# One layer of a hybrid encoder block on one core: TensorE's instructions fixed in program order, the recurrence's norm moved beside the next pair's chain, its output kept split, and the merge's gate blocks fetched ahead

## The chip, the core and the metric

The kernel runs on one core of a Trainium2 chip. The metric is the device time of one execution in microseconds. The kernel before took 1546.63 us (median of three runs, 1545.62 to 1550.25).

## What is computed

One layer over a sequence of 256 positions and a width of 2048, all in float32:

```
proj = rms_norm(x) @ w_in               # columns: SGU u, v | RWKV features | gate_a | gate_b
y_a  = sgu_mixer(u, v)                  # layer norm over 1024 columns, then 128x128 mixing per group
y_b  = rwkv_mixer(features)             # 16 heads of 64: a forward and a backward scan
       # o = group norm(o_f + o_b);  y_b = (o + bonus) * (sigmoid(g_lo) @ g2)
x    = x + (sigmoid(gate_a) * (y_a @ w_proj_a) + sigmoid(gate_b) * (y_b @ w_proj_b)) @ w_out
x    = x + (silu(conv3(rms_norm(x) @ w_gate)) * (rms_norm(x) @ w_up)) @ w_down
out  = rms_norm(x)
```

The scan is done in chunks of 64 positions: a 64x64 triangular system is inverted for each chunk, head and direction, and a short chain of small products carries the state from chunk to chunk.

## The kernel before

All large products run the same way. A weight tile (`raw`, 256 KB) comes from HBM; ScalarE rounds it (L271) and VectorE takes the remainder (L272), so that `hl` holds the weight as two parts; the activations are split in the same way. TensorE then issues, for each block of 128 weight rows, one matmul of 512 columns (L294) and one of 256 (L298). Four such pairs of matmuls make a chunk. `push` queues the chunks of a product, `advance(n)` issues the next n of them and splits the weights of three chunks ahead (`HL_AHEAD`), and `done` is what follows a product's last matmul: `evac_sum` takes the sum out of PSUM with one ScalarE copy (L310) and one VectorE addition (L311) into one of two `ev` buffers.

The small work is written as generators, and `run` lays chunks between their steps: a generator's `yield` says how much of the chunks should pass before its next step. The order is: the SGU (`sgu`), rates and operands of head pair 0, and then a loop over the pairs. In step p stand side by side the chain of pair p (`rwkv_chain`), the inverse of pair p+1 (`rwkv_inverse`) and the rates of pair p+2, and after them the norm of pair p (`rwkv_norm`) and the operands of pair p+2. `parts` splits a tile into `bs`, and `head_sums` (L642) sums it over a head with two matmuls into the one-bank PSUM tile `ms`. The large products between them are the projections and the gates; a gate block is written to DRAM by `keep` (L978, `spill`, through POOL's DMA queue).

This text is not the final order. A scheduler at build time moves instructions on every engine's queue, TensorE's included: where its cost table says that a small matmul's operand will not be ready, it takes a large matmul that stands later in the program. On the chip each engine then works its queue strictly in that order.

After the loop comes the merge: the outputs `yb` of the eight pairs are split into `ybs`, and for each of 16 column tiles `done_b` reads the gate block back (`sab`, L1070, through SP's queue), combines it and splits the result into `mg`. Then follow the output product, a norm (`sumsq_rstd`), the gate and up products and the down product.

Of the kernel before, what the change touches and what calls it, by code (L numbers as in the profile page):

```python
# [10 lines left out]
F32 = mybir.dt.float32  # L11
F32R = mybir.dt.float32r
I32 = mybir.dt.int32
AF = mybir.ActivationFunctionType
ALU = mybir.AluOpType
PSUM = bass.MemoryType.PSUM

P = 128
T = 256
D = 2048  # L20
KT = D // P
# [3 lines left out]
NP = RW // P  # L25
# [12 lines left out]

J0 = 4
WARM = 12  # L40
GY, TY, CY = 1.5, 2.5, 1.0
INV_Y = 4 * GY + 1.2 + 6 * TY + 2
CHAIN_Y = 12 * CY
SY = 1
NORM_Y = 3 + 2 * SY
# [74 lines left out]
    return out  # L120


@with_exitstack
def hybrid_kernel(ctx: ExitStack, tc: tile.TileContext, xT, w_in, w_pa, w_pb, w_out, w_g, w_u, w_d,
                  cols, consts, lora, sgu_wT, sgu_b, norm_f, out):
    nc = tc.nc
    V, A, PE, G = nc.vector, nc.scalar, nc.tensor, nc.gpsimd

    cpool = ctx.enter_context(tc.tile_pool(name="cpool", bufs=1))
    ps_mm = ctx.enter_context(tc.tile_pool(name="ps_mm", bufs=2, space=PSUM))  # L130
# [7 lines left out]
    def col(name, i):  # L138
        o, _ = COLS[name]
        return colt[:, o + i:o + i + 1]  # L140
# [41 lines left out]
    def split(dst, src):  # L182

        A.copy(dst[:, 0], src)
        V.tensor_tensor(out=dst[:, 1], in0=src, in1=dst[:, 0].bitcast(F32), op=ALU.subtract)
# [134 lines left out]
    drp = ctx.enter_context(tc.tile_pool(name="drp", bufs=1, space=bass.MemoryType.DRAM))  # L320
    es_mid, es_h, es_ya, es_f, es_h2, es_mg = (ExitStack() for _ in range(6))
    mid = es_mid.enter_context(tc.tile_pool(name="mid", bufs=1))
    hp = es_h.enter_context(tc.tile_pool(name="hp", bufs=1))
    fpool = es_f.enter_context(tc.tile_pool(name="fpool", bufs=1, side="right"))


    hp.tile([P, 8], F32, name="pad_h")
    h = [hp.tile([P, 2, T], F32R, name=f"h{k}") for k in range(KT)]
    hact = lambda k: h[k]
    yb = [mid.tile([P, T], F32, name=f"yb{p}") for p in range(NP)]  # L330


    fps = [fpool.tile([P, T + 2], F32, name=f"fp{i}") for i in range(2)]
# [276 lines left out]
    rp = es_r.enter_context(tc.tile_pool(name="rp", bufs=1, reuse_waits="tile"))  # L610
# [4 lines left out]
    rt = lambda name, shape, bufs=1: rp.tile([P] + shape, F32, name=name, tag=name, bufs=bufs)  # L615
# [30 lines left out]
    def rwkv_rates(p):  # L646

        k, v3, r, _ = feats[p]

        lr = rt("kd", [4, P])  # L650
        G.dma_start(lr, lora[p][:, 0:4])
        lgr = rt("Em", [4, P])[:, 0:2]
        G.dma_start(lgr, lora[p][:, 4:6])
        yield LY
        lw = rp.tile([P, 4, P], F32R, name="lw", tag="lw")
        A.copy(lw, lr)
        lg = rp.tile([P, 3, P], F32R, name="lg", tag="lg", bufs=3)
        A.copy(lg[:, 0::2], lgr)
        V.tensor_tensor(out=lg[:, 1], in0=lgr[:, 0], in1=lg[:, 0].bitcast(F32), op=ALU.subtract)
        V.tensor_tensor(out=lg[64:96, 2], in0=lgr[64:96, 1], in1=lg[64:96, 2].bitcast(F32), op=ALU.subtract)  # L660
        V.tensor_tensor(out=lw[C:P], in0=lr[C:P], in1=lw[C:P].bitcast(F32), op=ALU.subtract)
        yield 1
        tw = rt("tw", [2, T])
        ta = rt("ta", [2, T])
        for d in range(2):
            lp = ps_g.tile([P, 512], F32, name="gp", tag="gp")
            for i in range(2):
                for o in range(2):
                    PE.matmul(lp[:, i * T:(i + 1) * T], lw[:, 2 * i + d], xlo[i][d][:, o], start=(o == 0), stop=(o == 1))
            A.activation(tw[:, d], lp[:, 0:T], AF.Tanh, scale=0.5, bias=hb[:, d * NP + p:d * NP + p + 1])  # L670
            A.activation(ta[:, d], lp[:, T:2 * T], AF.Tanh, scale=0.5,
                         bias=hb[:, (2 + d) * NP + p:(2 + d) * NP + p + 1])
# [12 lines left out]
        ss = rt("hs", [T])
        ty = rt("tmp", [T], 3)
        kk = rt("kk", [T])
        A.activation(ss, k, AF.Square, scale=col("k_k", p))
        sp = parts(ss)
        yield SY  # L690
        sp = head_sums(sp)
        V.tensor_scalar(out=ss, in0=sp[:, 0:T], scalar1=1e-24, scalar2=None, op0=ALU.max)
        yield 1
        rsqrt(ty, ss, kk)
        V.scalar_tensor_tensor(out=kk, in0=k, scalar=col("k_k", p), in1=ty, op0=ALU.mult, op1=ALU.mult)
        yield 1
        bc = lambda a: a[:, None, :].to_broadcast([P, 2, T])

        kd = rt("kd", [4, P]).rearrange("p (d a) b -> p d (a b)", d=2)
        V.tensor_scalar(out=kd, in0=ta, scalar1=col("k_a", p), scalar2=ka2[:, p:p + 1], op0=ALU.mult, op1=ALU.add)  # L700
        V.tensor_tensor(out=kd, in0=kd, in1=bc(k), op=ALU.mult)
        V.scalar_tensor_tensor(out=ta, in0=ta, scalar=1.0, in1=bc(kk), op0=ALU.add, op1=ALU.mult)
        yield 1
        rates[p] = (L, Em, kk, kd, ta, lg)

    def rwkv_operands(p):

        k, v3, r, _ = feats.pop(p)
        L, Em, kk, kd, ta, lg = rates.pop(p)
        AR, PB = ARs[p % 2], PBs[p % 2]  # L710
        cv = lambda a: a.rearrange("p d (c j) -> p d c j", j=C)
        bcc = lambda a: a.rearrange("p (c j) -> p c j", j=C)[:, None].to_broadcast([P, 2, NC, C])
# [38 lines left out]
        V.tensor_tensor(out=bv.rearrange("p (a b) -> p a b", a=2), in0=bp[:, 0:T].rearrange("p (a b) -> p a b", a=2),  # L751
                        in1=v3f[:, :, 0:P], op=ALU.mult)
        yield 1
        heads[p] = (BK, UV, ZR, bv, lg)

    def rwkv_inverse(p):

# [41 lines left out]
        Tc = rt("Tc", [2, NC, 32], 2)  # L799
        V.transpose(out=Tc, in_=FQ[:, :, :, 1, :])  # L800
        keys_by_token(1)
        yield 1.2
        for l in range(2):
            xp = ps_t.tile([P, 512], F32, name="tp", tag="tp")
            xv = xp[:, 0:256].rearrange("p (d c k) -> p d c k", d=2, c=NC)
# [66 lines left out]
        yield 1  # L872

    def rwkv_chain(p):
        BK, UV, ZR, bv, lg = heads[p]
        Gs, Qf = solved.pop(p)
        AR, PB = ARs[p % 2], PBs[p % 2]

# [61 lines left out]
        outs[p] = O  # L940

    def rwkv_norm(p):
        BK, UV, ZR, bv, lg = heads.pop(p)
        O = outs.pop(p)

        mp = parts(O)
        yield SY
        mp = head_sums(mp)
        V.scalar_tensor_tensor(out=O, in0=mp[:, 0:T], scalar=-1.0 / C, in1=O, op0=ALU.mult, op1=ALU.add)
        yield 1  # L950
        sq2 = rt("tmp", [T], 3)
        A.activation(sq2, O, AF.Square)
        vp = parts(sq2)
        yield SY
        vp = head_sums(vp)
        ss2 = sq2
        ty2 = rt("tmp", [T], 3)
        tt2 = rt("tmp", [T], 3)
        V.tensor_scalar(out=ss2, in0=vp[:, 0:T], scalar1=1.0 / C, scalar2=GN_EPS, op0=ALU.mult, op1=ALU.add)
        yield 1  # L960
        rsqrt(ty2, ss2, tt2)
        V.tensor_tensor(out=O, in0=O, in1=ty2, op=ALU.mult)
        V.scalar_tensor_tensor(out=O, in0=O, scalar=col("gn_g", p), in1=bv, op0=ALU.mult, op1=ALU.add)
        gp2 = ps_ms.tile([P, 512], F32, name="ms", tag="ms")
        PE.matmul(gp2[:, 0:T], lg[:, 0], gsp[:, 0], start=True, stop=False)
        PE.matmul(gp2[:, 0:T], lg[:, 0], gsp[:, 1], start=False, stop=False)
        PE.matmul(gp2[:, 0:T], lg[:, 1], gsp[:, 0], start=False, stop=False)
        PE.matmul(gp2[:, 0:T], lg[0:96, 2], gst[0:96], start=False, stop=True)
        V.scalar_tensor_tensor(out=yb[p], in0=O, scalar=col("gn_b", p), in1=gp2[:, 0:T], op0=ALU.add, op1=ALU.mult)
        yield 1  # L970


    spill = {}
# [37 lines left out]
    for p in range(-1, NP):  # L1011
# [3 lines left out]
            pair_feats(p + 3)  # L1015
        push_fill(FILLS[p + 2])
        side, then = [], []
        if p >= 0:
            then.append((rwkv_norm(p), NORM_Y))
        if p < 0 or p + 1 == NP:  # L1020
            side.append((rwkv_inverse(p + 1), INV_Y) if p < 0 else (rwkv_chain(p), CHAIN_Y))
# [2 lines left out]
        if p + 2 < NP:  # L1024
# [11 lines left out]

    pools.update(raw=ctx.enter_context(tc.tile_pool(name="raw2", bufs=RAW2, reuse_waits="tile", side="right")),
                 ahead=RAW2 - 2)  # L1040
    xp_ = ctx.enter_context(tc.tile_pool(name="x2p", bufs=1, reuse_waits="tile", side="right"))
# [6 lines left out]
    h2 = [h2p.tile([P, 2, T], F32R, name=f"h2{m}") for m in range(KT)]  # L1048
    rstd2 = xp_.tile([P, T], F32, name="rstd2")
    mgr = es_mg.enter_context(tc.tile_pool(name="mgr", bufs=1, reuse_waits="tile", side="right"))  # L1050
    es_x = ExitStack()
    mgp = es_x.enter_context(tc.tile_pool(name="mgp", bufs=1, reuse_waits="tile"))
    mg = [mgr.tile([P, 2, T], F32R, name=f"mg{m}") for m in range(KT)]
    mgp.tile([P, 8], F32, name="pad_y")
    ybs = [mgp.tile([P, 2, T], F32R, name=f"ybs{p}") for p in range(NP)]
    for p in range(NP):
        split(ybs[p], yb[p])

    x2 = {}

    def load_x(m):
# [4 lines left out]
    def done_b(m, ps):  # L1066
        if m >= KT - X_AHEAD:
            load_x(m - KT + X_AHEAD)
        sab = mgp.tile([P, 2, T], F32, name="sab", tag="sab", bufs=4)
        nc.sync.dma_start(sab, spill[m])  # L1070
        sa, sb = sab[:, 0], sab[:, 1]
        V.scalar_tensor_tensor(out=sb, in0=sb, scalar=1.0, in1=evac_sum(ev, ps), op0=ALU.add, op1=ALU.mult)
        V.tensor_tensor(out=sa, in0=sa, in1=sb, op=ALU.add)
        split(mg[m], sa)
# [12 lines left out]
        last_d = push_tok(w_d[n], FT, lambda k: lt["act"][k], lambda t, ps, n=n: lt["d"](n, t, ps),  # L1087
                          LAG if n == ND - 1 else 0)
    finish(last_b)
    es_x.close()  # L1090
    es_mid.close()

    def sumsq_rstd(pool, dst, n_eps):
# [186 lines left out]
```

## Time and profile before

| | |
|---|---|
| median of three runs | 1546.63 us |
| the profiled execution | 1550.3 us |
| its span, first to last instruction | 1548.2 us |
| TensorE busy | 1525.0 us, 99% |
| VectorE busy | 1214.3 us, 78% |
| ScalarE busy | 925.0 us, 60% |
| granted TensorE clock, mean | 0.997 |

How to read it: TensorE's busy time includes the overlap of pipelined matmuls, so 99% does not mean that no time can be saved; the distance from one matmul's start to the next one's tells more. A wait is shown with the instruction that ended it.

### The profile page before, as it was taken

What the parts mean: (1) busy time and instruction counts of PE and PEld (TensorE: products, weight loads), DVE (VectorE), ACT (ScalarE), POOL (GpSimd) and SP (SyncE); (2) the same over time, 40 slices, a digit from 0 to 9 for tenths busy, and PEclk for the clock granted to TensorE, in tenths of its full rate; (3) what the DMA queues carried; (4) which work ended last, traced back from release to release, by engine and by line L of the source; (5) the groups of instructions that cost most, each with busy time, mean ns of one, the idle gap of its engine ahead of it and who ended that gap; (6) DMA issues with size and microseconds to landing.
All of it is one profiled execution on the core that took longest, in us unless ns stands there. A gap on an engine that the chain in (4) does not pass through costs nothing.

```text
span 1548.2 us, 34103 instructions
## 1 busy us (share of the span) xinstructions
PE 1525.0 (99%) x12680; PEld 1310.8 (85%) x12680; DVE 1214.3 (78%) x2496; ACT 925.0 (60%) x1946; POOL 38.1 (2%) x63
## 2 busy tenths in 40 slices
PE   9999999999999999989999999999999999999997
PEld 8888888888788878878888888888888888888886
DVE  8979998899889997678778777777777777555544
ACT  7767666665665664556665666665656666544442
POOL 0000000000000000000000000000000000000000
PEclk9999999999999999999999999999999999999999
DMA  8555453443443333587655555555555556766663
GB/s 282 187 176 186 155 165 123 132 133 133 134 141 121 125 100 129 178 272 244 207 189 183 189 191 190 190 189 192 190 190 188 192 188 217 230 193 194 194 175 110
DMA packets 148165, 274.65 MB, mean 177 GB/s; under 512 B 17056, under 2 KB 19232, under 8 KB 147872
## 3 DMA queue, kind: packets, MB, share of 16 engines
q1 hardware_dynamic: 145296, 265.14, 52.7%
q0 software_dynamic: 2560, 7.34, 1.5%
q8 instruction: 99, 1.62, 0.4%
q14 instruction: 66, 0.54, 0.1%
q10 hardware_dynamic: 144, 0.01, 0.0%
HBM read 266.13 MB, written 6.29 MB: 176 GB/s over the span
## 4 chain that ended last, share of the span: by engine, by line
PE 83%; issue 9%; DVE 4%; DMA 1%; ACT 1%; POOL 0%; SPq 0%; DVEq 0%; ACTq 0%; POOLq 0%
PE mm L294 40%; PE mm L298 21%; PE pd L232 5%; PE pd L230 5%; PE pd L231 5%; PE gp L770 1%; PE tp L818 1%; DVE hl L272 1%; PE ms L642 1%; DMA sab<-spill 1%; DVE FQ L796 1%; PE tp L808 1%; DMA spill<-ev 1%; PE cc L901 0%; ACT hl L271 0%
## 5 line engine op out<-in xcount | busy, mean ns | idle before, releaser
L294 PE MATMUL mm<-h,hl 128*128 128x512 f32 x2624 | 930.1, 395 | 0.0
L272 DVE TENSOR_TENSOR hl<-raw,hl 128x512 fp32r<-128x512 f32 x960 | 656.7, 691 | 218.9 <-ACT hl L271 215.5
L271 ACT CAST hl<-raw 128x512 fp32r<-128x512 f32 x960 | 593.5, 621 | 380.3 <-PE mm L298 162.8
L298 PE MATMUL mm<-h,hl 128*128 128x256 f32 x2624 | 740.6, 282 | 1.5 <-DVE hl L272 1.3
L294 PEld LDWEIGHTS mm<-h,hl 128*128 128x128 f32 x2624 | 492.8, 188 | 103.8
L298 PEld LDWEIGHTS mm<-h,hl 128*128 128x128 f32 x2624 | 495.9, 189 | 3.0 <-DVE hl L272 2.1
L310 ACT COPY ev<-mm 128x256 f32<-128x256 f32 x196 | 73.1, 373 | 125.2 <-PE mm L298 123.3
L231 PE MATMUL pd<-hl,act 128*128 128x512 f32 x352 | 136.9, 389 | 0.0
L230 PE MATMUL pd<-hl,act 128*128 128x512 f32 x352 | 136.9, 389 | 0.0
L232 PE MATMUL pd<-hl,act 128*128 128x512 f32 x352 | 136.9, 389 | 0.0
L311 DVE TENSOR_TENSOR ev<-mm,ev 128x256 f32<-128x256 f32 x196 | 82.9, 423 | 44.6 <-ACT ev L310 43.2
L294 PE MATMUL mm<-mg,hl 128*128 128x512 f32 x256 | 90.7, 395 | 0.0
L231 PEld LDWEIGHTS pd<-hl,act 128*128 128x128 f32 x352 | 66.1, 188 | 13.8
L232 PEld LDWEIGHTS pd<-hl,act 128*128 128x128 f32 x352 | 66.1, 188 | 13.8
L230 PEld LDWEIGHTS pd<-hl,act 128*128 128x128 f32 x352 | 66.1, 188 | 13.6
L298 PE MATMUL mm<-mg,hl 128*128 128x256 f32 x256 | 72.1, 282 | 0.0
L294 PEld LDWEIGHTS mm<-mg,hl 128*128 128x128 f32 x256 | 48.1, 188 | 9.6
L294 PE MATMUL mm<-ybs,hl 128*128 128x512 f32 x128 | 46.1, 401 | 4.0 <-DVE ev L311 3.4
L298 PEld LDWEIGHTS mm<-mg,hl 128*128 128x128 f32 x256 | 48.4, 189 | 0.0
L294 PE MATMUL mm<-ya,hl 128*128 128x512 f32 x128 | 47.7, 404 | 0.0
L1161 ACT ACTIVATE gt<-cp,colt 128x256 f32<-128x256 f32 x44 | 26.5, 602 | 19.4 <-DVE cp L1159 19.4
L298 PE MATMUL mm<-ybs,hl 128*128 128x256 f32 x128 | 36.8, 287 | 0.0
(292 smaller groups left out, 1430.5 us busy)
## 6 DMA issues: line engine op xcount, KB each, us to landing
raw<-in_w_in_dram SPq DMA_DIRECT2D x304, 256.0 KB, 2.9
raw<-in_w_g_dram SPq DMA_DIRECT2D x176, 256.0 KB, 2.7
raw<-in_w_u_dram SPq DMA_DIRECT2D x176, 256.0 KB, 2.8
raw<-in_w_d_dram SPq DMA_DIRECT2D x176, 256.0 KB, 3.0
raw<-in_w_out_dram SPq DMA_DIRECT2D x64, 256.0 KB, 3.0
raw<-in_w_pa_dram SPq DMA_DIRECT2D x32, 256.0 KB, 2.9
raw<-in_w_pb_dram SPq DMA_DIRECT2D x32, 256.0 KB, 4.3
spill<-ev POOLq DMA_DIRECT2D x32, 128.0 KB, 3.1
```

Source lines behind the costliest of these rows:

```text
L230: PE.matmul(ps, a[:, 0, ts], w[:, 0], start=(k == 0), stop=False)
L231: PE.matmul(ps, a[:, 0, ts], w[:, 1], start=False, stop=False)
L232: PE.matmul(ps, a[:, 1, ts], w[:, 0], start=False, stop=(k == nk - 1))
L271: A.copy(hl[:, 0, :m], raw[:, s0:s0 + m])
L272: V.tensor_tensor(out=hl[:, 1, :m], in0=raw[:, s0:s0 + m], in1=hl[:, 0, :m].bitcast(F32), op=ALU.subtract)
L294: PE.matmul(ps[:, 0:512], hl[:, 0, j], a.rearrange("p a t -> p (a t)"), start=(k == 0), stop=False)
L298: PE.matmul(ps[:, 0:256], hl[:, 1, j], a[:, 0], start=False, stop=(k == job["nk"] - 1))
L310: A.copy(t, ps[:, 256:512])
L311: V.tensor_tensor(out=t, in0=ps[:, 0:256], in1=t, op=ALU.add)
L642: PE.matmul(ps[:, 0:T], bones, b[:, o], start=(o == 0), stop=(o == 1))
L770: PE.matmul(gps[hh][:, c * P:(c + 1) * P], BK[rows, d, c, hh:hh + 2, :].rearrange("p a b -> p (a b)"), AR[rows, d, c].rearrange("p a b -> ...
L1161: A.activation(gt, b[:, 1:T + 1], AF.Identity, scale=col("cw1", f), bias=col("cb", f))
```

## The change

1. A class `InOrder` wraps `matmul` and `transpose`. Each TensorE instruction gets a dependency on the one before it, with no semaphore, so the scheduler keeps TensorE's queue in the order of the program. (All TensorE instructions now carry the line of the wrapper, L133.)
2. The norm of pair p no longer follows chain p; it runs in the next step, beside the chain of pair p+1. The norm of the last pair still follows its chain.
3. The norm writes its result to `O` and splits it at once into `ybs[p]`; the merge no longer splits eight tiles. The 256 KB of gate LoRA weights (`lgr`) are fetched and split in the norm instead of in the rates.
4. The gate blocks for the merge are fetched on POOL's queue instead of SP's, three tiles ahead, from a pool that is opened when the pairs' pools close. The DMA scratch is set to 8192 bytes.
5. Two steps of the inverse get other weights for `run`: 1.25 instead of 1.5 for each of the four products at its start, and 2.2 instead of 1.2 after the first transposition.

```
-GY, TY, CY = 1.5, 2.5, 1.0
-INV_Y = 4 * GY + 1.2 + 6 * TY + 2
+GY, TY, CY = 1.25, 2.5, 1.0
+INV_Y = 4 * GY + 2.2 + 6 * TY + 2
...
+class InOrder:
...
+    def _next(self, op, *args, **kw):
+        tc = self.tc
+        traced = tc.nc.cur_bb.bb.instructions
+        n = len(traced)
+        op(*args, **kw)
+        for ins in traced[n:]:
+            if self.last is not None:
+                tc.add_manual_dep(
+                    ins, self.last.name,
+                    mybir.DependencyInfo(mybir.DependencyClass.NoSync, mybir.DependencyReason.DATA),
+                    reason="order")
+            self.last = ins
...
-    V, A, PE, G = nc.vector, nc.scalar, nc.tensor, nc.gpsimd
+    V, A, G = nc.vector, nc.scalar, nc.gpsimd
+    PE = InOrder(tc)
...
-    yb = [mid.tile([P, T], F32, name=f"yb{p}") for p in range(NP)]
+    ybs = [mid.tile([P, 2, T], F32R, name=f"ybs{p}") for p in range(NP)]
...
     def rwkv_norm(p):
+        bv = heads.pop(p)[3]
         O = outs.pop(p)
+        lgr = rt("lgr", [2, P])
+        G.dma_start(lgr, lora[p][:, 4:6])
...
-        V.scalar_tensor_tensor(out=yb[p], in0=O, scalar=col("gn_b", p), in1=gp2[:, 0:T], op0=ALU.add, op1=ALU.mult)
+        V.scalar_tensor_tensor(out=O, in0=O, scalar=col("gn_b", p), in1=gp2[:, 0:T], op0=ALU.add, op1=ALU.mult)
+        split(ybs[p], O)
...
-        if p >= 0:
+        if p > 0:
+            side.append((rwkv_norm(p - 1), NORM_Y))
+        if p == NP - 1:
             then.append((rwkv_norm(p), NORM_Y))
...
+    def load_sab(m):
+        if m < KT:
+            sab[m] = sap.tile([P, 2, T], F32, name="sab", tag="sab", bufs=4)
+            G.dma_start(sab[m], spill[m])
+
+    for m in range(3):
+        load_sab(m)
...
-    for p in range(NP):
-        split(ybs[p], yb[p])
...
-        sab = mgp.tile([P, 2, T], F32, name="sab", tag="sab", bufs=4)
-        nc.sync.dma_start(sab, spill[m])
-        sa, sb = sab[:, 0], sab[:, 1]
+        load_sab(m + 3)
+        s_ = sab.pop(m)
+        sa, sb = s_[:, 0], s_[:, 1]
```

What the scheduler makes of it shows in TensorE's queue. First place: the mean of the SGU's layer norm (`ms<-acc`), which follows the last of the eight v products. `h_96` to `h_111` are the 16 blocks of one product. TensorE before:

```order
L294 MATMUL mm<-h_99,hl 128x512
L298 MATMUL mm<-h_99,hl 128x256
L294 MATMUL mm<-h_100,hl 128x512
L298 MATMUL mm<-h_100,hl 128x256
L294 MATMUL mm<-h_101,hl 128x512
L298 MATMUL mm<-h_101,hl 128x256
L294 MATMUL mm<-h_102,hl 128x512
L298 MATMUL mm<-h_102,hl 128x256
L472 MATMUL ms<-acc,cst 128x256
```

TensorE of the change, at the same `ms<-acc`:

```order
L133 MATMUL mm<-h_110,hl 128x512
L133 MATMUL mm<-h_110,hl 128x256
L133 MATMUL mm<-h_111,hl 128x512
L133 MATMUL mm<-h_111,hl 128x256
L133 MATMUL ms<-acc,cst 128x256
L133 MATMUL mm<-h_96,hl 128x512
L133 MATMUL mm<-h_96,hl 128x256
```

Before, 14 large matmuls of the next product (blocks 96 to 102) stood ahead of the sum; now it stands directly behind the product that feeds it. In the whole queue, 270 large matmuls stood ahead of it and now 256; ahead of the first transposition of the SGU (`sgt`) 375 and now 352; ahead of the last sum of the second norm (`ms<-sqn`) 3463 and now 3456; ahead of the first `ms<-bs` of pair 0's operands 880 and now 872. In the loop over the pairs, the small products that follow an operand from VectorE or ScalarE have up to 7 large matmuls fewer ahead of them in a step with an odd pair, and up to 11 fewer in one with an even pair, counted from the step's first large matmul.

Second place: where the chain of one pair (`cc`, `oc`), the products at the start of the next pair's inverse (`gp<-AR,BK`) and the norm's sums meet. TensorE before:

```order
L889 MATMUL cc<-ZR,Gs 64x64 x3
L642 MATMUL ms<-bs,bones 128x256
L889 MATMUL cc<-ZR,Gs 64x64
L770 MATMUL gp<-AR_1689,BK 128x128 x2
L642 MATMUL ms<-bs,bones 128x256
L770 MATMUL gp<-AR_1689,BK 128x128 x5
L965 MATMUL ms<-gsp,lg 128x256
L966 MATMUL ms<-gsp,lg 128x256
L967 MATMUL ms<-gsp,lg 128x256
L968 MATMUL ms<-gst,lg 128x256
L770 MATMUL gp<-AR_1689,BK 128x128
```

TensorE of the change, there:

```order
L133 MATMUL mm<-ya_134,hl 128x512
L133 MATMUL mm<-ya_134,hl 128x256
L133 MATMUL cc<-ZR,Gs 64x64 x4
L133 MATMUL gp<-AR_1689,BK 128x128 x8
L133 MATMUL mm<-h_96,hl 128x512
L133 MATMUL mm<-h_96,hl 128x256
```

Groups of one kind now stand together. Over the whole queue, 214 stretches of small matmuls between large ones became 180, 328 changes of the tile shape (128x128, 64x128, 128x64, 64x64, 32x32) became 279, and `gp<-AR,BK` comes in 16 pieces instead of 31.

Third place: POOL's queue at the merge, DMA alone. `spill` followed by a number is one gate block in DRAM. POOL before:

```order
L978 DMA spill_9354<-ev 128x256 x2
L978 DMA spill_9591<-ev 128x256 x2
L978 DMA spill_9796<-ev 128x256 x2
L978 DMA spill_10069<-ev 128x256 x2
L1152 MEMSET cp_11858 128x258
```

POOL of the change:

```order
L1006 DMA spill_9572<-ev 128x256 x2
L1006 DMA spill_9806<-ev 128x256
L1076 DMA sab<-spill_2218 128x512
L1076 DMA sab<-spill_2937 128x512
L1076 DMA sab<-spill_3658 128x512
L1006 DMA spill_9806<-ev 128x256
L1076 DMA sab<-spill_3958 128x512
L1006 DMA spill_10066<-ev 128x256 x2
L1076 DMA sab<-spill_4828 128x512
```

The last three writes of gate blocks now stand behind three and four fetches of 256 KB each.

## Rows read from the trace of the kernel before

**Rows 1.** The page: busy us of the engines, share of the span, instructions

```profile
PE 1525.0 (99%) x12680; PEld 1310.8 (85%) x12680; DVE 1214.3 (78%) x2496; ACT 925.0 (60%) x1946; POOL 38.1 (2%) x63
```

**Rows 2.** Window in the pairs: length, busy us of each engine, clock, DMA share, GB/s

```profile
520.00:540.00 20.00, 19.94 (x226) 16.03 (x226) 18.02 (x46) 12.27 (x34) 0.54 (x1) 1.00 0.27 95
```

**Rows 3.** Timeline of TensorE in the pairs: start us, duration, line, tiles

```profile
279.31 0.39 PE L294 MATMUL mm<-ya,hl 128*128 128x512 f32 x1
279.76 0.38 PE L642 MATMUL ms<-bs,bones 128*128 128x256 f32 x1
279.98 0.28 PE L298 MATMUL mm<-ya,hl 128*128 128x256 f32 x1
280.10 0.39 PE L294 MATMUL mm<-ya,hl 128*128 128x512 f32 x1
280.32 0.28 PE L642 MATMUL ms<-bs,bones 128*128 128x256 f32 x1
280.44 0.28 PE L298 MATMUL mm<-ya,hl 128*128 128x256 f32 x1
...
281.72 0.38 PE L642 MATMUL ms<-bs,bones 128*128 128x256 f32 x1
282.03 0.33 PE L889 MATMUL cc<-ZR,Gs 64*64 64x64 f32 x2
...
284.97 0.50 PE L294 MATMUL mm<-h,hl 128*128 128x512 f32 x1
285.31 0.28 PE L298 MATMUL mm<-h,hl 128*128 128x256 f32 x1
285.43 0.39 PE L294 MATMUL mm<-h,hl 128*128 128x512 f32 x1
285.66 0.28 PE L298 MATMUL mm<-h,hl 128*128 128x256 f32 x1
```

**Rows 4.** Waits of TensorE, by line and releaser: total us, times, longest

```profile
PE tp L808 <- DVE Tc L800: 3.0, 5, 0.9
...
PE gp L770 <- DVE BK L720: 1.1, 1, 1.1
```

**Rows 5.** Timeline of TensorE at the merge: matmuls that waited

```profile
663.25 0.38 PE L298 MATMUL mm<-h,hl 128*128 128x256 f32 x1 [1.32 <-DVE hl L272]
...
668.02 0.47 PE L294 MATMUL mm<-ybs,hl 128*128 128x512 f32 x1 [0.57 <-DVE ybs L185]
...
679.97 0.64 PE L294 MATMUL mm<-ybs,hl 128*128 128x512 f32 x1 [3.39 <-DVE ev L311]
```

**Rows 6.** Timeline at the SGU's mean and at its first transposition

```profile
54.94 0.42 DVE L415 TENSOR_TENSOR acc<-acc,vu 128x256 f32<-128x256 f32 x1
55.42 0.70 PE L472 MATMUL ms<-acc,cst 128*128 128x256 f32 x2
...
74.31 1.09 ACT L494 ACTIVATE vu<-vu,colt 128x256 f32<-128x256 f32 x2
74.97 0.44 PE L497 MATMUL sgt<-cst,vu 128*128 128x128 f32 x2
```

**Rows 7.** Timeline at pair 0's first products and operands; [wait <-releaser]

```profile
169.77 0.49 PE L770 MATMUL gp<-AR,BK 64*128 64x128 f32 x2 [1.07 <-DVE BK L720]
...
172.84 0.41 DVE L185 TENSOR_TENSOR bs<-hs,bs 128x256 fp32r<-128x256 f32 x1
```

**Rows 8.** Window of 4 us behind the wait of 3.39 us at the merge

```profile
680.00:684.00 4.00, 4.00 (x14) 3.42 (x15) 3.22 (x8) 1.32 (x3) 0.00 (x0) 0.57 0.72 222
```

**Rows 9.** The chain that ended last, at the merge: start, us, transfer

```profile
654.14 7.93 DMA spill<-ev
...
668.38 9.19 DMA sab<-spill
```

**Rows 10.** Timeline of VectorE: the multiplication for the last gate block

```profile
662.17 0.42 DVE L982 TENSOR_TENSOR ev<-ev,rstd 128x256 f32<-128x256 f32 x1 [3.76 <-DMA spill<-ev]
```

**Rows 11.** POOL's writes of gate blocks: shortest/mean/longest ns, first and last start

```profile
L978 POOL DMA_DIRECT2D spill<-ev x32: 539/539/547, 173.9 to 672.7; - x32
```

More of the change, by code (lines that the diff above doesn't have):

```diff
@@ L120, in build_constants, with __init__, matmul, transpose @@
     return out
+class InOrder:
+    def __init__(self, tc):
+        self.tc, self.last = tc, None
+    def _next(self, op, *args, **kw):
[10 more added lines that the diff above has]
+            self.last = ins
+    def matmul(self, *args, **kw):
+        self._next(self.tc.nc.tensor.matmul, *args, **kw)
+    def transpose(self, *args, **kw):
+        self._next(self.tc.nc.tensor.transpose, *args, **kw)
 @with_exitstack
@@ L322, in hybrid_kernel @@
     mid = es_mid.enter_context(tc.tile_pool(name="mid", bufs=1))
+    mid.tile([P, 8], F32, name="pad_h")
     hp = es_h.enter_context(tc.tile_pool(name="hp", bufs=1))
     fpool = es_f.enter_context(tc.tile_pool(name="fpool", bufs=1, side="right"))
-    hp.tile([P, 8], F32, name="pad_h")
     h = [hp.tile([P, 2, T], F32R, name=f"h{k}") for k in range(KT)]
     hact = lambda k: h[k]
-    yb = [mid.tile([P, T], F32, name=f"yb{p}") for p in range(NP)]
+    ybs = [mid.tile([P, 2, T], F32R, name=f"ybs{p}") for p in range(NP)]
     fps = [fpool.tile([P, T + 2], F32, name=f"fp{i}") for i in range(2)]
@@ L651, in rwkv_rates @@
         G.dma_start(lr, lora[p][:, 0:4])
-        lgr = rt("Em", [4, P])[:, 0:2]
-        G.dma_start(lgr, lora[p][:, 4:6])
         yield LY
@@ L656, in rwkv_rates @@
         A.copy(lw, lr)
[L657 to L660, printed above, removed]
         V.tensor_tensor(out=lw[C:P], in0=lr[C:P], in1=lw[C:P].bitcast(F32), op=ALU.subtract)
@@ L703, in rwkv_rates @@
         yield 1
-        rates[p] = (L, Em, kk, kd, ta, lg)
+        rates[p] = (L, Em, kk, kd, ta)
     def rwkv_operands(p):
         k, v3, r, _ = feats.pop(p)
-        L, Em, kk, kd, ta, lg = rates.pop(p)
+        L, Em, kk, kd, ta = rates.pop(p)
         AR, PB = ARs[p % 2], PBs[p % 2]
@@ L753, in rwkv_operands @@
         yield 1
-        heads[p] = (BK, UV, ZR, bv, lg)
+        heads[p] = (BK, UV, ZR, bv)
     def rwkv_inverse(p):
@@ L801, in rwkv_inverse @@
         keys_by_token(1)
-        yield 1.2
+        yield 2.2
         for l in range(2):
@@ L874, in rwkv_chain @@
     def rwkv_chain(p):
-        BK, UV, ZR, bv, lg = heads[p]
+        BK, UV, ZR, bv = heads[p]
         Gs, Qf = solved.pop(p)
@@ L942, in rwkv_norm @@
     def rwkv_norm(p):
-        BK, UV, ZR, bv, lg = heads.pop(p)
+        bv = heads.pop(p)[3]
         O = outs.pop(p)
+        lgr = rt("lgr", [2, P])
+        G.dma_start(lgr, lora[p][:, 4:6])
         mp = parts(O)
@@ L962, in rwkv_norm @@
         V.tensor_tensor(out=O, in0=O, in1=ty2, op=ALU.mult)
+        lg = rp.tile([P, 3, P], F32R, name="lg", tag="lg", bufs=1)
+        A.copy(lg[:, 0::2], lgr)
+        V.tensor_tensor(out=lg[:, 1], in0=lgr[:, 0], in1=lg[:, 0].bitcast(F32), op=ALU.subtract)
+        V.tensor_tensor(out=lg[64:96, 2], in0=lgr[64:96, 1], in1=lg[64:96, 2].bitcast(F32), op=ALU.subtract)
         V.scalar_tensor_tensor(out=O, in0=O, scalar=col("gn_g", p), in1=bv, op0=ALU.mult, op1=ALU.add)
@@ L1035, in hybrid_kernel @@
     es_h.close()
+    sap = ctx.enter_context(tc.tile_pool(name="sap", bufs=1, reuse_waits="tile", side="right"))
+    sab = {}
+    def load_sab(m):
[4 more added lines that the diff above has]
+        load_sab(m)
     pools.update(raw=ctx.enter_context(tc.tile_pool(name="raw2", bufs=RAW2, reuse_waits="tile", side="right")),
@@ L1050, in hybrid_kernel @@
     mgr = es_mg.enter_context(tc.tile_pool(name="mgr", bufs=1, reuse_waits="tile", side="right"))
-    es_x = ExitStack()
-    mgp = es_x.enter_context(tc.tile_pool(name="mgp", bufs=1, reuse_waits="tile"))
     mg = [mgr.tile([P, 2, T], F32R, name=f"mg{m}") for m in range(KT)]
-    mgp.tile([P, 8], F32, name="pad_y")
-    ybs = [mgp.tile([P, 2, T], F32R, name=f"ybs{p}") for p in range(NP)]
-    for p in range(NP):
-        split(ybs[p], yb[p])
     x2 = {}
@@ L1089, in hybrid_kernel @@
     finish(last_b)
-    es_x.close()
     es_mid.close()
@@ L1268 @@
     laid = _lay_out(inputs)
-    nc = bacc.Bacc("TRN2", target_bir_lowering=False, num_devices=1)
+    nc = bacc.Bacc("TRN2", target_bir_lowering=False, num_devices=1, dynamic_dma_scratch_size=8192)
     arrays, args = {}, {}
```

## The prediction

> **What bounds the kernel now.** I read the page's busy times first: TensorE works 1525.0 of 1548.2 us, VectorE 78%, ScalarE 60% [rows 1]. TensorE sets the end, so an edit can pay in two ways only: TensorE's work becomes cheaper, or it waits less. Next I read the windows, because 78% is a mean: in the loop over the pairs VectorE is busy 18.02 of 20 us [rows 2], so there an operand that TensorE needs early can come late. Third, the timeline of TensorE gives the prices. From one 512-column matmul to the next one with nothing between takes 0.34 us (284.97, 285.31, 285.43, 285.66: the steps are 0.34, 0.12, 0.23, and the steady pair is 0.12 + 0.23 = 0.35); one large matmul is thus worth 0.173 us [rows 3]. Fourth, the waits: TensorE's largest are a handful, 3.39, 3.0 in five, 1.32, 1.1, 0.57 us [rows 4, 5]. So hardly anything is left to win in waits outside the merge, and the change touches a queue that hides them well.
>
> **A. Fewer interruptions: a gain.** A stretch of small matmuls costs more than its own columns. A single sum laid inside a pair: 279.31 to 279.98 is 0.67 us, without it 0.23, and the sum itself 0.12, so 0.32 lost; the same at 280.10 to 280.44 is 0.34, which loses nothing. On the way back from small shapes the first pair step is 0.34 (284.97 to 285.31) where 0.23 is steady, 0.11 lost at that end alone [rows 3]. The diff's 214 stretches become 180: 34 fewer. I take 0.30 each, near the 0.32, as most of them also change the tile shape: 10.2 us. Inside the stretches a foreign group costs too: 281.72 to 282.03 is 0.31 for a sum of 0.12 columns' time, 0.19 lost; `gp<-AR,BK` comes in 15 pieces fewer: 15 x 0.19 = 2.9. Sum A = -13.1. Ends: 49 fewer shape changes at the 0.11 of one end alone, -5.4; the same 49 at the 0.32 of a whole visit, -15.7.
>
> **B. Waits that the old order covered: a loss.** Program order takes away large matmuls that stood ahead of small ones. Where the small one came just as its operand did, each of them is now a wait of 0.173 us.
> - The SGU. Before, `acc` was ready at 54.94 + 0.42 = 55.36 and `ms<-acc` ran at 55.42; the first `sgt` ran at 74.97 behind ScalarE's `vu`, two in 1.09 us from 74.31, so the first was ready near 74.86 [rows 6]. Both came just in time with 14 and 23 large matmuls more ahead of them. The 23 include the 14: 23 x 0.173 = +4.0 us. Ends: 2.4 (only the 14) and 4.0.
> - The last sum of the second norm, 7 fewer: +1.2 (0 to 1.2).
> - Pair 0. `gp<-AR,BK` waited until 169.77, and the sum's `bs` was ready at 172.84 + 0.41 = 173.25, 3.5 us later [rows 7]; now `ms<-bs` stands 8 large matmuls (1.4 us) earlier and ahead of work that could have filled the time. What queues behind it is all of TensorE. Between 1.4 and 3.5 + 1.5 = 5.0; I take +2.5.
> - The steps of the pairs: 7 or 11 large matmuls fewer, 1.2 or 1.9 us, if the operand comes as late as before; the mean 1.55 over seven steps is 10.8 us. Nothing, if VectorE and ScalarE run ahead by as much. VectorE is 90% busy there [rows 2], nearer to the upper end, but the norm's work no longer stands between a chain and the next step. I take +6 (0 to 10.8).
>
> Sum B = 4.0 + 1.2 + 2.5 + 6 = +13.7, ends 3.8 and 21.0 with all terms at one end.
>
> **C. The merge: a gain, in part given back.** [...] The `sab` fetch was issued late (its 9.19 us are on the chain [rows 9]); three fetches ahead remove that wait, and with it the slow clock: -5.0. The split of `ybs` is done for seven pairs of eight: -0.5. The 1.32 stays, and may grow: VectorE waited 3.76 us [rows 10] until a write of an older gate block had landed, 7.93 us after its issue [rows 9], since there are two `ev` buffers. Now the last three writes stand behind three or four fetches of 256 KB on the same queue. If these add nothing, 0; if the write waits for one more such landing, 9.19 - 7.93 + 3.76 = 5.0 us more on VectorE, whose splits TensorE then lacks. I take +2.5. C = -3.0, ends -6.9 and -0.5.
>
> In the trace POOL's 32 issues took 539 to 547 ns each, with VectorE 78% busy [rows 1, 11]. [...]
>
> **E. The rest.** The waits for `Tc`, 3.0 us in five [rows 4], meet a `yield` of 2.2 instead of 1.2: -1.0 (0 to -3.0). A wait of some 5 us at pair 0 may lower the clock as the 3.39 did, 1.6 us at half odds: +0.7. The gate LoRA weights' fetch and two splits per pair move to another step with nothing near that waits: 0. The `ybs` splits move from the merge into the loop, 16 operations on engines with 10% free at VectorE [rows 2]: in B's range.
>
> **Sum:** -13.1 + 13.7 - 3.0 - 1.0 + 0.7 = -2.7 us. The profiled execution took 1550.3 us (span 1548.2 and 2.1 around it), 3.7 above the median of the runs; the change comes off the median: 1546.6 - 2.7 = 1544.
>
> **Rivals.**
> 1. Faster: the engines run ahead, so the waits of B are covered (its low end, 3.8, plus 2 for pair 0 and clock), and the merge is freed wholly (-6.9). -13.1 + 5.8 - 6.9 - 1.0 = -15: 1531. For it: the norm beside the next chain gives VectorE's operands a step more time. Against: VectorE at 90% [rows 2].
> 2. Slower: in-order waits in the pair steps. One mechanism: a small product at TensorE's head waits for VectorE with all large ones behind it. At 1.9 us in each of eight steps it costs 15 instead of 6, and A gives only 9.3, the middle of 13.1 and its lower end: -2.7 + 9 + 3.8 = +10: 1557; it decides from about 12 us of waits before `ms`, `gp` and `cc` in the pairs. Half of that, 1552, is slower already.
> 3. POOL's queue: the fetches are not ahead, because they and the gate blocks' writes hold each other up; the merge's 6.9 stay lost, with 2.5 on top in the last gate blocks: -13.1 + 13.7 + 2.5 - 0.3 = +3: 1549. [...]
> 4. The change doesn't do what it says: the scheduler's order is not fixed. The queue as listed is in the program's order, so this has no chance of its own.
>
> **How the numbers follow.** A measurement of this kernel tells about 0.3% (4.6 us) from no change: below 1542.0 is faster, above 1551.3 slower. The forecast has 0.42, with 1538 to 1550 as its own range: 0.12 of it below 1542. Rival 1 has 0.30, nearly all faster (0.27). Rival 2 has 0.18, of it 0.15 slower. Rival 3 has 0.10, of it 0.04 slower. So faster 0.39, slower 0.19, same 0.42. The range must reach most of rival 1 and half of rival 2: 1531 to 1554.
>
> **What the profile of the changed kernel would show.** A: the busy TensorE time between waits is less by some 13 us, and the step into and out of stretches stays at 0.2 to 0.3. B: waits of TensorE before `ms<-acc` near 52 us (2.4), `sgt` near 72 (1.6), pair 0's `ms<-bs` (3 to 5), `ms<-sqn` (1.2), and in the pairs 6 us in all; none there means rival 1, 12 or more rival 2. C: no wait for the first `sab`, a granted clock of 1.00 behind it, and a wait of VectorE for a `spill` write longer than 3.76; if `sab` is waited for still, rival 3. I am wrong if the stretches' price does not fall with their number, or if one wait that is not in this list is over 5 us.

## The result and the profile after

The changed kernel took 1556.88 us (median of four runs, 1554.5 to 1560.07) against 1546.12 us before: a ratio of 1.0066, 95% interval 1.004 to 1.0092. It is slower by some 10 us; the prediction was 2.7 us faster, and its range ended at 1554.

The page's busy times of the changed kernel, to be read beside [rows 1]:

```profile
PE 1517.0 (98%) x12680; PEld 1307.5 (84%) x12680; DVE 1213.1 (78%) x2496; ACT 923.8 (59%) x1946; POOL 46.7 (3%) x79
```

Its span is 1552.7 us. TensorE works 8.0 us less than before, and the rest of the span, in which it does nothing, grew from 1548.2 - 1525.0 = 23.2 to 35.7 us, by 12.5. So the gain is there, and a larger loss beside it: +4.5 in the profiled execution. The other three runs were longer still, with spans of 1555.3, 1554.9 and 1558.3 us at a mean granted clock of 0.993, 0.993 and 0.992, where the profiled one had 0.995. The two profiles thus show a little under half of the 10.8 us between the medians. The profiled execution of the changed kernel is 2.4 us below its median, and that part goes with the clock; the profiled execution of the kernel before is 4.1 us above its own median, and no run here says why.

The waits of TensorE in the changed kernel, by releaser (total us, times, longest), to be read beside [rows 4]:

```profile
PE ms L133 <- ACT bs L211: 11.5, 8, 3.8
PE mm L133 <- DVE hl L299: 2.8, 3, 2.1
PE ms L133 <- DVE acc L442: 2.6, 1, 2.6
PE sgt L133 <- ACT vu L521: 1.9, 1, 1.9
PE ms L133 <- DVE on L564: 1.6, 1, 1.6
PE ms L133 <- ACT sqn L1132: 1.4, 1, 1.4
PE cc L133 <- DVE ZR L949: 1.3, 2, 0.7
PE ms L133 <- DVE bs L212: 0.9, 2, 0.5
PE cc L133 <- ACT Z L916: 0.6, 1, 0.6
```

The wait of the first norm (`on`, 1.6) is the same before, though the prediction's list of the largest waits leaves it out. None of the other small products in this list waited more than 0.5 us in all before, and `Tc`, 3.0 us in [rows 4], is gone from it. The timeline of TensorE shows three of them, at the SGU's mean, at pair 0's operands and at a pair's operands; they answer to [rows 6, 7]:

```profile
56.02 0.87 PE L133 MATMUL ms<-acc,cst 128*128 128x256 f32 x2 [2.56 <-DVE acc L442]
...
179.35 1.08 PE L133 MATMUL ms<-bs,bones 128*128 128x256 f32 x2 [3.81 <-ACT bs L211]
...
407.51 0.85 PE L133 MATMUL ms<-bs,bones 128*128 128x256 f32 x2 [1.14 <-ACT bs L211]
408.20 1.55 PE L133 MATMUL mm<-ya,hl 128*128 128x512 f32 x8
```

The last two rows are the mechanism in two lines: TensorE stands for 1.14 us before a sum, and the large matmuls that it then runs needed nothing of that sum.

The clock, in windows of 5 us (columns as in [rows 2]; the granted clock is the third number from the end), at the SGU's mean, at pair 0 and at the merge:

```profile
55.00:60.00 5.00, 3.98 (x13) 3.39 (x14) 3.49 (x10) 1.62 (x4) 0.00 (x0) 0.66 0.34 115
175.00:180.00 5.00, 1.19 (x6) 0.66 (x4) 5.00 (x12) 2.52 (x6) 0.54 (x1) 0.93 0.37 122
180.00:185.00 5.00, 5.00 (x31) 4.09 (x32) 4.04 (x9) 2.25 (x5) 0.45 (x1) 0.73 0.58 197
665.00:670.00 5.00, 3.33 (x19) 2.66 (x18) 0.63 (x2) 0.31 (x2) 0.00 (x0) 1.00 0.71 267
670.00:675.00 5.00, 4.55 (x17) 3.87 (x18) 3.99 (x8) 2.86 (x7) 0.54 (x1) 0.66 0.65 208
```

Three times a wait, of 2.56, 3.81 and 2.1 us, is followed by a stretch of lower granted clock: 0.50 in windows of 1 us from 57 to 59, from 180 to 182 and from 671 to 674 us. Estimated from the windows above as (1 - clock) x 5 us, these cost 1.7, 0.35 + 1.35 and 1.7 us, 5.1 in all, against 1.6 for the one place before, where 14 matmuls ran in 4.00 us [rows 8] and 23 would fit at 0.173 us each [rows 3].

At the merge, VectorE's timeline and the chain of waits; they answer to [rows 9, 10]:

```profile
669.37 0.42 DVE L1010 TENSOR_TENSOR ev<-ev,rstd 128x256 f32<-128x256 f32 x1 [4.55 <-DMA spill<-ev]
```

```profile
660.55 8.73 DMA spill<-ev
```

No wait for `sab` is left. But the write of a gate block took 8.73 us from issue to landing, VectorE stood 4.55 us behind it, and TensorE 2.1 us behind VectorE's weight split.

To see where the time went I also read, from both traces, when the same large matmul starts (there are 7328, in the same order in both). The k-th one is later than before by 0.36 us at k = 240 (50.2 us before), 6.35 at 480, 9.44 at 960, 6.41 at 2640, 3.03 at 2880, 4.53 at 3480, and stays at 4.53 to the end. So: the SGU +6.0, pair 0 +3.1, the steps of the pairs -3.0, the merge -3.4, the second norm +1.5.

### The profile page after: what moved, and what is told of

Its sections match the earlier page's. It is cut to its first block, busy times and chain, and to the rows that moved or that the text cites. A ratio compares the mean times of both kernels' runs of the same rounds, so it can differ in the third digit from the quotient of the medians.

```text
span 1552.7 us, 34106 instructions
## 1 busy us (share of the span) xinstructions
PE 1517.0 (98%) x12680; PEld 1307.5 (84%) x12680; DVE 1213.1 (78%) x2496; ACT 923.8 (59%) x1946; POOL 46.7 (3%) x79
## 4 chain that ended last, share of the span: by engine, by line
PE 82%; DVE 11%; ACT 2%; issue 2%; DMA 2%; POOL 0%; SPq 0%; DVEq 0%; ACTq 0%
PE mm L133 60%; PE pd L133 15%; DVE hl L299 3%; PE gp L133 2%; PE tp L133 1%; PE cc L133 1%; DMA raw<-in_w_in_dram 1%; PE ms L133 1%; DVE ev L338 1%; ACT hl L298 1%; DMA spill<-ev 1%; PE oc L133 0%; DVE ZR L949 0%; DVE tmp L207 0%; DVE st L947 0%
## 5 line engine op out<-in xcount | busy, mean ns | idle before, releaser
L133 PE MATMUL mm<-h,hl 128*128 128x512 f32 (+1 forms) x5248 | 951.3, 339 | 2.7 <-DVE hl L299 2.3
L133 PEld LDWEIGHTS mm<-h,hl 128*128 128x128 f32 x5248 | 807.6, 189 | 109.8 <-DVE hl L299 3.4
L133 PE MATMUL pd<-hl,act 128*128 128x512 f32 x1056 | 239.5, 389 | 0.0
L133 PEld LDWEIGHTS pd<-hl,act 128*128 128x128 f32 x1056 | 198.1, 188 | 41.1
L133 PE MATMUL mm<-mg,hl 128*128 128x512 f32 (+1 forms) x512 | 92.1, 338 | 0.0
L133 PEld LDWEIGHTS mm<-mg,hl 128*128 128x128 f32 x512 | 78.6, 188 | 9.7
L133 PE MATMUL mm<-ya,hl 128*128 128x512 f32 (+1 forms) x256 | 51.8, 346 | 0.5 <-DVE hl L299 0.5
L133 PEld LDWEIGHTS mm<-ya,hl 128*128 128x128 f32 x256 | 40.1, 193 | 5.9 <-DVE hl L299 0.8
L133 PE MATMUL mm<-ybs,hl 128*128 128x512 f32 (+1 forms) x256 | 44.8, 336 | 0.0
L133 PEld LDWEIGHTS mm<-ybs,hl 128*128 128x128 f32 x256 | 39.3, 188 | 5.3 <-DVE ev L338 0.3
L133 PE MATMUL ms<-bs,bones 128*128 128x256 f32 x64 | 16.8, 325 | 12.8 <-ACT bs L211 11.5
L133 PEld LDWEIGHTS ms<-bs,bones 128*128 128x128 f32 x64 | 10.5, 191 | 18.3 <-ACT bs L211 14.0
L1195 DVE SCALAR_TENSOR_TENSOR gt<-cp,colt,gt 128x256 f32<-128x256 f32 x44 | 21.3, 484 | 3.2
```

The lines of the kernel that those rows point to most:

```text
L133: op(*args, **kw)
L1195: V.scalar_tensor_tensor(out=gt, in0=b[:, 0:T], scalar=col("cw0", f), in1=gt, op0=ALU.mult, op1=ALU.add)
```

## The experiments

Theory W: program order exposes waits that the scheduler had covered with large matmuls, and the clock falls behind the longer ones. Rivals: order is neutral, and the norm's place or POOL's queue loses the time. Times are medians; the kernel before had 1546.7, 1547.4 and 1547.5 us in the three groups of runs (e1 to e4, e5 to e8, e9 and e10).

**e1, only the order.** To the kernel before:

```
-    V, A, PE, G = nc.vector, nc.scalar, nc.tensor, nc.gpsimd
+    V, A, G = nc.vector, nc.scalar, nc.gpsimd
+    PE = InOrder(tc)
```

Expected: 

> The kernel before with TensorE in program order and nothing else of the change. Theory W (program order exposes waits that the scheduler's order covered, above all in the SGU, at pair 0's operands and at the second norm, and the granted clock falls behind the long ones): slower than before by 8 to 14 us, with TensorE waits before ms<-acc, sgt and pair 0's ms<-bs as in the changed kernel, and a granted clock of 0.995 or less. Rival N (order is neutral or a gain, the loss comes from the norm's new place or from POOL's queue): within 4 us of before, or faster.

Measured: 1566.66 us, ratio 1.013 (1.0115 to 1.0145): +20 us, well above W's range, and rival N falls. TensorE's queue has 183 stretches of small matmuls instead of 212 (a count that leaves out two at the start; the changed kernel has 178 by it), and TensorE's busy time falls only from 1525.0 to 1521.7 us, while the time in which it does nothing rises from 23.2 to 40.8. The clock fell in two places:

```profile
175.00:180.00 5.00, 3.64 (x16) 2.77 (x18) 4.26 (x11) 3.20 (x8) 0.54 (x1) 0.73 0.80 252
180.00:185.00 5.00, 5.00 (x37) 4.44 (x36) 4.86 (x13) 1.57 (x3) 0.55 (x1) 0.93 0.36 119
570.00:575.00 5.00, 3.27 (x62) 2.18 (x61) 4.75 (x12) 3.74 (x10) 0.00 (x0) 0.83 0.14 47
575.00:580.00 5.00, 5.00 (x18) 4.17 (x17) 3.13 (x8) 3.95 (x12) 0.00 (x0) 0.50 0.33 105
```

By the same working that is some 5 us against 1.6, so at equal clock the busy time fell by some 6.5 us, 0.2 us for each of 29 stretches. `acc`, `vu` and pair 0's `bs` wait 2.3, 1.9 and 3.8 us, much as in the changed kernel. But in the loop over the pairs TensorE waits 16.4 us, against 10.7 in the changed kernel, and the largest of these waits are others:

```profile
PE ms L133 <- DVE bv L778: 4.6, 6, 1.0
PE ms L133 <- DVE O L976: 3.1, 6, 0.5
PE ms L133 <- DVE tmp L986: 1.7, 4, 0.7
```

In this kernel's code the three VectorE operations read a sum out of `ms`, whose pool has one buffer, so the next sum waits for the tile; two of them belong to the norm, which here still follows its own chain.

**e2, all but the order.** In the changed kernel:

```
-    PE = InOrder(tc)
+    PE = nc.tensor
```

Expected: 

> The changed kernel with the scheduler's own order for TensorE again, everything else of the change kept. Theory W: the SGU's and pair 0's waits are gone, the merge's 3.4 us are still won: 1540 to 1546 us, no slower than before. Rival N: the loss stays, 1553 to 1558 us.

Measured: 1536.14 us, ratio 0.9934 (0.992 to 0.9947), better than W's range. So order costs some 20 us with the rest of the change as without it (1556.9 - 1536.1 = 20.7), and the rest is a gain of 10.6. That the two costs are alike does not make them the same waits, as e1's list shows. All five runs lie within 1535.2 to 1537.5 at clocks of 0.997 and 0.998.

**e3, order from the loop over the pairs on.** The wrapper adds its dependencies only after pair 0's operands:

```
+    PE.on = True
     for p in range(-1, NP):
```

Expected: 

> The changed kernel in which program order holds only from the loop over the pairs on; the SGU and pair 0's operands are ordered by the scheduler. Theory W with the loss ahead of the loop: SGU 6 and pair 0 some 3 us come back, and with them the clock: 1543 to 1548 us. Rival W2 (waits in the steps of the pairs are the larger part): 1552 to 1556 us.

Measured: 1547.57 us, ratio 1.0002 (0.9991 to 1.0013). Of the 20.7 us, 9.3 come from ahead of the loop (1556.9 to 1547.6) and 11.4 from the loop and what follows (to 1536.1). The time lies in the range of "the loss ahead of the loop", near its upper end, but neither half alone is the loss: W holds in both, and W2's "larger part" is right by a little, though its range was missed. Its eleven runs spread from 1543.3 at a clock of 0.998 to 1550.6 at 0.994.

**e4, no fetch ahead.** In the changed kernel, `done_b` fetches its own gate block on SP's queue:

```
-            G.dma_start(sab[m], spill[m])
+            nc.sync.dma_start(sab[m], spill[m])
...
-    for m in range(3):
-        load_sab(m)
...
-        load_sab(m + 3)
+        load_sab(m)
```

Expected: 

> The changed kernel with the merge's gate blocks fetched as before: on SP's queue, each when its tile is combined, none ahead. If the fetch ahead wins what the traces show between the last pair and the second tile of the merge (3.4 us with the splits of ybs): 1559 to 1562 us, and a wait of TensorE of some 3 us at the first tile. Rival Q (fetches on POOL's queue delay the last writes and cost what they win): 1553 to 1557 us.

Measured: 1552.69 us, ratio 1.0037 (1.0025 to 1.005). The first expectation was wrong: leaving the fetch ahead out is 4.2 us faster than having it. Q's range was missed by 0.3 us, but its reading fits: the fetch ahead costs more than it wins. The windows show TensorE at the merge without a gap (those of the changed kernel stand above):

```profile
665.00:670.00 5.00, 5.00 (x31) 4.45 (x30) 3.70 (x9) 3.40 (x8) 0.00 (x0) 1.00 0.98 359
670.00:675.00 5.00, 5.00 (x31) 4.41 (x30) 3.14 (x6) 2.14 (x4) 0.54 (x1) 1.00 0.85 266
```

The expected wait for the first `sab` is not there either. The issues of `sab`, from the kernel before and then from e4 (shortest, median, longest ns; first and last start in us), show the reason:

```profile
L1070 SPq DMA_DIRECT2D sab<-spill x16: 326/327/604, 668.4 to 712.0; - x16
```

```profile
L1076 SPq DMA_DIRECT2D sab<-spill x16: 326/327/813, 662.2 to 710.3; - x16
```

With no fetch ahead in the program, the first one is issued 6.2 us earlier than before, since SP runs ahead of the work that needs it: the first operation on that tile starts at 677.2, 15 us after the issue. Before, the tile lay in a pool of the merge with `ybs`; here it has its own, opened earlier. That the pool held the fetch back is read from the code and not tried by itself.

**e5, the scheduler's order and no fetch ahead**: the edits of e2 and e4 together. Expected: 

> The scheduler's order for TensorE, and the gate blocks fetched on SP's queue as before, none ahead; norm, split output and yields as in the changed kernel. If the fetches on POOL's queue cost what the run without them won in program order (1556.9 to 1552.7): 1531 to 1534 us against 1536.1 with them. Rival: in the scheduler's order the fetch ahead costs nothing or helps (TensorE's waits at the merge are only 0.9 us there): 1535 to 1540 us.

Measured: 1532.95 us, ratio 0.9901 (0.9887 to 0.9914). The fetch ahead on POOL's queue costs 3.2 us in the scheduler's order too. This is the fastest version, faster than both kernels.

**e6, the fetch ahead on SP's queue.** In the changed kernel:

```
-            G.dma_start(sab[m], spill[m])
+            nc.sync.dma_start(sab[m], spill[m])
```

Expected: 

> The changed kernel, in program order, with the gate blocks still fetched three ahead but on SP's queue. If the harm is that the last writes of gate blocks stand behind the fetches on one queue: VectorE's waits for a spill write fall from 4.55 to about 1 us and the time is that without the fetch ahead, 1551 to 1554 us. Rival: fetching early is itself the harm (the transfers share the 16 engines with the weights, whichever queue issues them, or SP's queue waits for the writes before it issues the weights): 1555 to 1562 us.

Measured: 1553.13 us, as without any fetch ahead (1552.69). VectorE's waits for a `spill` write are 1.45 and 1.00 us instead of 4.55 and 2.17:

```profile
667.27 0.43 DVE L1010 TENSOR_TENSOR ev<-ev,rstd 128x256 f32<-128x256 f32 x1 [1.45 <-DMA spill<-ev]
```

So the harm is the fetches on POOL's queue, not the early transfer. The first three fetches, issued in the changed kernel from 658.7 us on and in e6 from 659.4 on, and their times to landing:

```profile
L1076 POOL DMA_DIRECT2D sab<-spill x3: 536/541/541, 658.7 to 659.8; - x3
DMA to landing us min/median/max: 7.0/7.7/9.0
```

```profile
L1076 SPq DMA_DIRECT2D sab<-spill x3: 330/382/382, 659.4 to 660.3; - x3
DMA to landing us min/median/max: 3.2/3.4/3.6
```

Whether it is the order of one queue or the way in which POOL's transfers start, e6 does not separate: it changes both.

**e7, the norm behind its own chain**, in the scheduler's order (edit of e2):

```
-        if p > 0:
-            side.append((rwkv_norm(p - 1), NORM_Y))
-        if p == NP - 1:
+        if p >= 0:
             then.append((rwkv_norm(p), NORM_Y))
```

Expected: 

> The scheduler's order, and the norm of a pair behind its own chain again; all else as in the changed kernel. TensorE's queue has 214 stretches of small matmuls here and 191 with the norm beside the next chain, 332 and 299 changes of tile shape. At 0.3 us for a stretch, as the prediction took it: 23 x 0.3 = 7 us slower than the scheduler's order with the norm moved, so 1542 to 1545 us, TensorE's busy time some 7 us more. Rival (a stretch costs little, the gain of 10 us is the merge's and the yields'): 1535 to 1539 us.

Measured: 1547.79 us, 11.7 more than e2. The pages of e7 and of e2:

```profile
PE 1524.4 (99%) x12680; PEld 1309.6 (85%) x12680; DVE 1213.9 (79%) x2496; ACT 926.4 (60%) x1946; POOL 46.8 (3%) x79
```

```profile
PE 1515.2 (99%) x12680; PEld 1306.3 (85%) x12680; DVE 1210.6 (79%) x2496; ACT 922.3 (60%) x1946; POOL 46.7 (3%) x79
```

With spans of 1546.0 and 1533.5 us, 9.2 of 12.5 us are TensorE's busy time, both at a mean clock of 0.998. Put on the 23 stretches fewer it is 0.40 us each, above the 0.3 expected and twice the 0.2 of e1: a stretch has no one price, and what else the norm's place makes cheaper was not tried. The norm's new place alone is as large as the gain of e2 (10.6), and it is bought without program order.

**e8, the old yields**, in the scheduler's order: `GY` 1.5 and `yield 1.2`. Expected: 

> The scheduler's order, and the inverse's old weights for the chunks between its steps (1.5 and 1.2 instead of 1.25 and 2.2); all else as in the changed kernel. If the yield of 2.2 is what took away the waits for Tc (3.0 us in before, none after): 1538 to 1541 us with those waits back. Rival (other steps moved them): 1535 to 1538 us.

Measured: 1537.27 us, 1.1 more than e2, with runs that overlap, and one wait of 0.4 us for `Tc`. The rival is right: with the norm moved these waits are gone whatever the yields are.

**e9, program order with large matmuls laid by hand** where it waited, and no fetch ahead (edit of e4):

```
     def sgu():
+        yield 1
         ps = ps_ms.tile([P, 512], F32, name="ms", tag="ms")
...
         rsqrt(rs, sv, tv)
-        yield 1
+        yield 2
...
         bp = parts(ks)
-        yield SY
+        yield SY + 1
         bp = head_sums(bp)
...
-        yield 1
         heads[p] = (BK, UV, ZR, bv)
...
-    run([(sgu(), 22.0)], SGU_CHUNKS)
+    run([(sgu(), 24.0)], SGU_CHUNKS)
```

Expected: 

> Program order as in the changed kernel and no fetch ahead, but the program itself lays large matmuls ahead of the small products that waited: two chunks (16 matmuls) ahead of the SGU's first sum, one more share ahead of its first transposition (376 instead of 352 ahead of it), and one chunk (8) more ahead of the sum in the operands of each pair. If the missing large matmuls are the loss: the waits for acc and vu are gone, pair 0's falls by 1.4 us or more, those for bs at the pairs' operands too, and the time comes from 1552.7 us (program order, no fetch ahead) to 1538 to 1544 us. Rival (program order costs for another reason, such as the order that the scheduler gives the other engines with it): no less than 1549 us.

Measured: 1540.08 us, ratio 0.9953 (0.9939 to 0.9967), 12.6 less than e4. Its first waits:

```profile
PE ms L133 <- ACT bs L211: 2.8, 2, 2.0
PE mm L133 <- DVE hl L299: 2.7, 4, 1.7
PE ms L133 <- DVE on L565: 1.6, 1, 1.6
PE ms L133 <- ACT sqn L1130: 1.4, 1, 1.4
```

`vu` is gone from the list and `acc` of L442 with it; the waits for `bs` at the operands of the pairs fell from eight to two by 8 large matmuls each. So most of what program order costs (12.6 of 19.7 us, e4 less e5) is the missing large matmuls. The time still lacks 7 us to e5, and the profiles show where: TensorE does nothing for 23.0 us against 16.9, and the granted clock fell in two places (0.50 from 175 to 180 us, 0.80 from 565 to 570), in e5 at neither.

**e10, the kept split alone**: the edits of e5, e7 and e8 together, which leaves the output written split and kept, the gate LoRA weights in the norm, and `sab`'s own pool. Expected: 

> Of the change only the output written split and kept and the gate LoRA weights in the norm: the scheduler's order, the norm behind its own chain, the old yields, the gate blocks fetched on SP's queue with none ahead. By the differences of the runs so far (norm back 1547.8, fetch ahead 3.2, yields 1.1 us): 1544 to 1547 us, no difference from before or slightly faster. Rival (the kept splits are worth the merge's wait by themselves): 1538 to 1542 us.

Measured: 1545.31 us, ratio 0.999 (0.9981 to 0.9998): 2.2 us less than its kernel before by the medians, 1.5 by the ratio, whose interval lies close to 1.

Laid end to end: kept split -2.2 (e10), norm beside the next chain -11.7 (e7 to e2), yields -1.1 (e8 to e2), fetch ahead on POOL's queue +3.2 (e5 to e2), program order +20.7 (e2 to the changed kernel). The sum is +8.9; the changed kernel measured +10.8. The parts come from different groups of runs and are good to a microsecond or so each.

## Why the prediction was wrong

The prediction's answer for the whole was the small difference of a gain A and a loss B, and B was sized too low: 13.7 us taken, 4.5 + 1.4 + 3.8 + 10.5 = 20.2 in the list of waits, and with them 1.7 + 1.7 us of lower clock at the SGU and pair 0, where the prediction had 0.7 in all. The mechanism of B was right. Step by step:

- **A, -13.1 from fewer stretches: the size nearly held, the price did not.** The busy time fell by 8.0 us although 5.1 instead of 1.6 us were lost to the lower clock, so by 11.5 at equal clock. The 0.30 for a stretch came from one of two visits in [rows 3], of which the other lost nothing, and the runs give no one price: 0.40 by e7 and e2, 0.2 by e1. At equal clock program order alone wins some 6.5 us and the norm's place alone 9.2, which do not add up either: both together gave the 11.5. By putting both edits into one term, the prediction never asked what program order was worth by itself.
- **B, the step that failed.** The SGU's 4.0 us of waits came out as 2.6 + 1.9 = 4.5, with 1.7 us of lower clock behind the first, which had no term. Pair 0 was 3.8 of wait and 1.7 of clock; part of it came back soon after, +3.1 against 2.5 + 0.7. The second norm's 1.2 was 1.4. The steps of the pairs were taken at 6 of 10.8 us, because VectorE and ScalarE would run ahead by some of it. They did not: by the list of waits above, the waits there are 11.5 - 3.8 for `bs` from ScalarE, 0.9, 1.3 and 0.6, 10.5 us in all, the upper end. The reading "VectorE is 90% busy", 18.02 of 20 us [rows 2], was right. The reason given for staying below it, that the norm no longer stands in the way, was worth something: in e1, which lacks the norm's move and the rest of the change, the waits in the loop are 16.4 us against 10.7. But what it lowered was larger than the 10.8 taken.
- **Outside the profiled execution** another 2 to 6 us are lost with a clock of 0.993 and 0.992. The prediction gave the clock one term of 0.7 us at one place. That these runs lose the clock behind the same waits in more places is likely, and e2 and e5, with few waits, hardly lose it; but no trace of them was kept, so it isn't shown.
- **C, -3.0: right in the sum by luck, wrong in its cause.** The merge gave -3.4. The first `sab` wait went, and VectorE waited 4.55 instead of 3.76 us for the write behind the fetches. The prediction saw this return but priced it at 2.5 beside a gain of 5.0 that it credited to the fetch ahead. The 5.0 is the wait of 3.39 us [rows 5] and the 1.6 us estimated above for the clock of 0.57 behind it [rows 8]; with the waits of 1.32 and 0.57 us [rows 5] they make its 6.9, and E's 0.7 is half odds on the 1.6. In e4, without the fetch ahead, the same comparison of starts gives -7.6 over the merge: gain and return were both larger than taken, and their errors cancel. The gain comes from the kept splits and the tile's own pool together, and on POOL's queue the fetch ahead only costs: 4.2 us. POOL's issues stayed at 536 to 552 ns in the changed kernel, but its first three fetches landed after 7.0 to 9.0 us, and those on SP's queue after 3.2 to 3.6 (e6). What makes POOL's fetches land later no run here shows; on SP's queue the same fetches made the kernel some 4 us faster (e6).
- **E.** The waits for `Tc` went wholly (-3.0 instead of -1.0), through the norm's place and not the yield (e8).
- **The rivals.** Rival 2 named 1557 and the mechanism that decided, with a chance of 0.18; in the pairs its 12 us of waits were 10.5, and pair 0, the SGU and the clock did the rest. That its number is right to a microsecond is luck: it had 15 us in the pairs, and a gain A of 9.3.

## What to carry to other kernels

Where a scheduler has slid independent work ahead of small products, count for each of them how much work it slid, and take the product of count and duration as the cost of taking that away, in full, where an engine that makes the operand is some 90% busy, as it came here (10.5 of 10.8 us); the clock that falls behind the waits comes on top (here an estimated 5.1 us against 1.6 before). Then lay the same work there by hand, or leave that queue to the scheduler. And price each edit by itself: here a gain of some 12 us sat unseen beside a loss of 20, and one experiment for each (e2, e7) was enough to see it.

## What was not expected of the hardware

TensorE's granted clock fell behind a wait of only 2.56 us (to 0.66 in the window from 55 to 60 us), but the length of the wait alone does not decide it: in e4 the same product waited 2.59 us, in e6 2.3, and the clock of that window stayed at 1.00. e4's rows:

```profile
56.09 0.70 PE L133 MATMUL ms<-acc,cst 128*128 128x256 f32 x2 [2.59 <-DVE acc L442]
...
55.00:60.00 5.00, 3.91 (x22) 3.46 (x23) 4.17 (x12) 2.61 (x8) 0.00 (x0) 1.00 0.33 109
```

Two runs of one kernel can differ by some microseconds, with a lower mean clock in the longer one (e3: 1543.3 at 0.998, 1550.6 at 0.994). Waits do not foretell this spread: e4, with the waits of the changed kernel but the merge's, lies within 2.1 us over five runs, and the kernel before, with few, spreads over 5.4 us in sixteen.

On POOL's queue, a write of 128 KB behind fetches of 256 KB took 8.73 us to land, where the median of the 32 was 2.9. With the fetches on SP's queue (e6) the same write, the third from last, took 5.6 us, and VectorE's wait for it fell from 4.55 to 1.45. The fetches are not all of it: before, with writes alone on POOL's queue, this write took 7.93 us [rows 9].
